# Differential attention: the eight transposes of a query block in one run instead of two groups

## The chip, the cores and the metric

The kernel runs on one core of a Trainium2 chip. The time is the device time of one execution in microseconds (us); where several executions were timed, the median stands for them. The engines are named as in the profile: PE (the matrix engine), PEld (PE's weight loads), DVE (the vector engine), ACT (the scalar engine), POOL and SP (which issues most transfers).

## The reference

A trunk of two layers works on `x` of 1024 positions by 1024 channels. Layer 0 mixes by pooling, layer 1 by differential attention; each is followed by a gated feed-forward part, and a last norm closes it. The change lies in the attention of layer 1, which has 8 heads of two 64-wide halves:

```
sc = jnp.einsum('bqhce,bkhce->bhcqk', qb, k).astype(jnp.float32)
p = jax.nn.softmax(sc, axis=-1)
a = p[:, :, 0] - lam * p[:, :, 1]
return jnp.einsum('bhqk,bkhe->bqhe', a.astype(v.dtype), v)
...
o = _rms_norm(o, subln, DIFF_SUBLN_EPS) * (1.0 - lam_init)
return o.reshape(b, s, h * 2 * dh) @ w_o
```

## The kernel before

Every matrix is split into a high and a low part, and a product is the sum of three products (high by high, high by low, low by high). Names that end in `_hi` and `_lo` are these parts: `_hi` is a rounded copy (L131, on ACT), `_lo` the difference (L132, on DVE).

The attention runs over 8 heads of 8 query blocks of 128 rows, one block a step: 64 steps, and 2 more to drain. A step holds these pieces, each a letter in a string:

- `s`, `S` (`score_mm`): the scores of the first and the second softmax of this block, four matmuls each into a 1024-wide `sc` (L1130); then DVE takes the row maximum (L1132, and a small addition at L1134 for the first), and ACT the exponential with its sum (`prob`, L1135).
- `c` (`combine`): DVE takes a reciprocal (L1141), a factor `cc` (L1143), and puts the two softmaxes together in two halves of 512 columns (L1146).
- `a`, `b` (`a_prep`): the first and the second half of the combined block **of the step before** are transposed on PE, four transposes of 128x128 each (`aT`, L1161), into one PSUM buffer a half; ACT and DVE read it into `a_hi` and `a_lo`.
- `p` (`pv`): on every second step, the product of two blocks with the values (`po`, L1172, 24 matmuls). Its first half needs the halves `a`, its second the halves `b`.
- `t` (`o_turn`): `po` is copied (L1187), transposed (`oT`, L1190), copied (L1191) and squared (L1196).
- `m`, `f`, `F`: the norm of the head before. `m` scales with `rr` (L1210, L1211; the product at L1213 is on POOL), `f` and `F` transpose its output, four transposes each (`oT2`, L1230), only at step 3 of a head.
- `q` (`score_q`): the query parts of the next step, `q_hi` on ACT and `q_lo` on POOL.
- `.`: two matmuls `pj` of the next head's projections (L1041, L1083), in the last head three of the output projection (L1268).

All small transposes and `po` share one PSUM pool of two buffers (tag `tr`): a group waits until the buffer before last has been read.

`PLAN` gives the pieces of an even and an odd step of heads 0 to 6, `PLAN7` those of head 7, the last. The loop is

```
with tc.manual_schedule(engines={mybir.EngineType.PE}):
    for g in range(H * NT + 2):
        j, i = divmod(g, NT)
        pj, pi = divmod(g - 1, NT)
        for step in (PLAN7 if j == H - 1 else PLAN)[g % 2]:
```

so the strings set the order of PE alone. The order of DVE, ACT, POOL and SP is laid out by a scheduler before the run, with its own costs and with priorities that the pieces carry: 20 for the scores and `a_prep`, 50 for `combine` and `o_turn`, 100 for `f` and `F`. Each engine then works through its list in that order.

Of the kernel before, what the change touches and what calls it, by code (L numbers as in the profile page):

```python
# [25 lines left out]
NT = S // P  # L26
NK = D // P
ORDER = (0, 4, 1, 5, 2, 6, 3, 7)
PLAN = ("...saq.bS..c.p", "st.aS.m.q.fb....F.c..")
PLAN7 = (".as.b....S.pqc.", "tmsaSqcb..f......F..")  # L30
AHEAD = 3
WQ, RQ = 14, 3
PB = (2, 1)
# [56 lines left out]
def trunk_kernel(  # L90
# [1233 lines left out]

    assert sum(p.count('.') for p in PLAN) == 18
    done = []
# [4 lines left out]
# [5 lines that stand above are left out]
                if step == ".":  # L1336
# [128 lines left out]
```

## Time and profile before

| | us |
|---|---|
| median of three runs | 2075.68 (2073.62 to 2076.55) |
| the profiled execution | 2073.84 |
| its span, first to last instruction | 2072.0 |
| PE busy | 1998.1 (96%) |
| DVE busy | 1557.2 (75%) |
| ACT busy | 1023.2 (49%) |
| POOL busy | 890.8 (43%) |

The profile is one execution. A row of the timeline has the start, the length in us, the engine, the line and the operation, output from inputs, and, in brackets, how long the engine had been idle and whose end it then followed. A row of waits has the engine and its instruction, the releaser, the us in total, how often, and the longest. The attention steps lie between about 783 and 1350 us; a head's eight steps take 70.4 us, and the steps shown in the prediction (1 to 4 of head 2) begin near 929 us.

### The profile page before, as it was taken

Reading aid. Unit: us, or ns where it says so; the run is one execution under the profiler, and the core shown is the slowest. Engines: PE = TensorE matmul, PEld = TensorE weight load, DVE = VectorE, ACT = ScalarE, POOL = GpSimd, SP = SyncE. Lnnn points to the kernel's source line nnn. Section 1 sums busy time; section 2 is a strip of 40 time slices with the busy share of each in tenths; the row PEclk is TensorE's granted clock in tenths of the full one; section 3 lists DMA queues with packets and bytes.
Section 4 is the critical chain, followed back from the end, with each engine's and each line's share of the span. In section 5 each row is a group of like instructions: output and inputs, shape, how many; then the busy total and the mean of one; then the engine's idle time right before and its main releaser. Section 6 shows DMA issues by size and latency. Waiting matters only on the chain.

```text
span 2072.0 us, 27643 instructions
## 1 busy us (share of the span) xinstructions
PE 1998.1 (96%) x9659; PEld 1664.6 (80%) x9659; DVE 1557.2 (75%) x2286; ACT 1023.2 (49%) x1838; POOL 890.8 (43%) x676
## 2 busy tenths in 40 slices
PE   6699999999999999999999998998999999999998
PEld 6678888888888877888888887876888888888886
DVE  7867777777675658999889988767776777775665
ACT  7733333333453646666667666565433333344343
POOL 4499999996000000101110111015999999930000
PEclk8899999999999999999999999998999999999999
DMA  4325454454976522122212115263445445458663
GB/s 172 104 91 176 138 192 140 158 173 129 378 226 209 193 66 67 43 70 65 64 44 74 56 42 188 102 195 111 130 140 193 147 158 177 138 196 336 201 213 131
DMA packets 221720, 301.90 MB, mean 146 GB/s; under 512 B 17852, under 2 KB 142092, under 8 KB 218764
## 3 DMA queue, kind: packets, MB, share of 16 engines
q1 hardware_dynamic: 221580, 300.13, 44.4%
q8 instruction: 76, 1.25, 0.3%
q14 instruction: 64, 0.52, 0.1%
HBM read 196.78 MB, written 90.70 MB: 139 GB/s over the span
## 4 chain that ended last, share of the span: by engine, by line
PE 87%; DVE 7%; ACT 3%; issue 1%; DMA 1%; SPq 1%; DVEq 0%; ACTq 0%
PE dn L610 19%; PE up_b L436 17%; PE up_c L436 11%; PE up_a L436 11%; PE pj L1041 7%; PE sc L1130 5%; PE pj L1083 4%; PE po L1172 3%; PE aT L1161 3%; PE pj L1268 2%; DVE nm L1132 1%; PE pp L862 1%; ACT prob L1135 1%; PE pl L842 1%; PE wo_acc L1268 1%
## 5 line engine op out<-in xcount | busy, mean ns | idle before, releaser
L1112 POOL TENSOR_TENSOR q_lo<-qt,q_hi 128x256 fp32r<-128x256 f32 x64 | 50.0, 781 | 679.7 <-ACT q_hi L1111 362.2
L394 POOL TENSOR_TENSOR w_lo<-s,w_hi 128x512 fp32r<-128x512 f32 x168 | 269.4, 1604 | 19.4 <-ACT w_hi L393 19.1
L610 PE MATMUL dn<-hnT_hi 128*128 128x512 f32 x560 | 218.3, 390 | 0.0
L610 PE MATMUL dn<-hnT_hi,hnT_lo 128*128 128x512 f32 x560 | 218.1, 389 | 0.0
L610 PE MATMUL dn<-hnT_lo,hnT_hi 128*128 128x512 f32 x560 | 218.1, 389 | 0.0
L436 PE MATMUL up_b<-x_hi,w_hi 128*128 128x512 f32 x528 | 207.5, 393 | 5.0 <-ACT x_hi L318 4.1
L436 PE MATMUL up_b<-x_lo,w_hi 128*128 128x512 f32 x528 | 207.3, 393 | 1.7 <-DVE x_lo L319 1.7
L394 POOL TENSOR_TENSOR w_lo<-raw,w_hi 128x512 fp32r<-128x512 f32 x130 | 194.7, 1499 | 30.8 <-ACT w_hi L393 30.2
L436 PE MATMUL up_b<-x_hi,w_lo 128*128 128x512 f32 x528 | 206.8, 392 | 0.0
L393 ACT CAST w_hi<-s 128x512 fp32r<-128x512 f32 x176 | 108.7, 618 | 178.0 <-PE up_b L436 90.0
L1132 DVE TENSOR_REDUCE nm<-sc 128x1 f32<-128x1024 f32 x128 | 155.8, 1218 | 14.4 <-PE sc L1130 14.0
L593 ACT CAST hnT_hi<-mst 128x1024 fp32r<-128x1024 f32 (+1 forms) x76 | 74.6, 982 | 168.6 <-PE dn L610 128.7
L594 DVE TENSOR_TENSOR hnT_lo<-mst,hnT_hi 128x1024 fp32r<-128x1024 f32 (+1 forms) x76 | 86.5, 1139 | 91.0 <-ACT hnT_hi L593 90.8
L1135 ACT ACTIVATE prob<-sc,nm 128x1024 f32<-128x1024 f32 x128 | 142.7, 1115 | 23.1 <-DVE nm L1132 11.6
L436 PE MATMUL up_a<-hnT_hi,w_hi 128*128 128x512 f32 x352 | 139.2, 396 | 5.3 <-ACT g L513 4.7
L436 PE MATMUL up_a<-hnT_lo,w_hi 128*128 128x512 f32 x352 | 138.6, 394 | 0.1
L436 PE MATMUL up_a<-hnT_hi,w_lo 128*128 128x512 f32 x352 | 138.3, 393 | 0.0
L408 POOL TENSOR_TENSOR s<-raw 128x512 f32<-128x512 f32 x84 | 133.3, 1587 | 11.6 <-DMA raw<-in_ffn_w_up_dram 4.2
L436 PE MATMUL up_c<-hnT_hi,w_hi 128*128 128x512 f32 x352 | 137.3, 390 | 0.0
L436 PE MATMUL up_c<-hnT_hi,w_lo 128*128 128x512 f32 x352 | 137.1, 389 | 0.0
L436 PE MATMUL up_c<-hnT_lo,w_hi 128*128 128x512 f32 x352 | 137.1, 389 | 0.0
L393 ACT CAST w_hi<-raw 128x512 fp32r<-128x512 f32 x132 | 81.6, 618 | 84.8 <-PE up_c L436 76.4
(320 smaller groups left out, 5448.9 us busy)
## 6 DMA issues: line engine op xcount, KB each, us to landing
raw<-in_ffn_w_up_dram SPq DMA_DIRECT2D x88, 512.0 KB, 4.4
mst<-m_dram SPq DMA_DIRECT2D x70, 512.0 KB, 6.2
wd<-in_ffn_w_down_dram SPq DMA_DIRECT2D x22, 1024.0 KB, 6.0
wd_dram<-wd SPq DMA_DIRECT2D x22, 1024.0 KB, 6.4
m_dram<-cm SPq DMA_DIRECT2D x80, 256.0 KB, 5.8
wst<-wd_dram SPq DMA_DIRECT2D x40, 512.0 KB, 5.2
m_dram<-gc SPq DMA_DIRECT2D x66, 256.0 KB, 6.3
wst<-in_ffn_w_down_dram SPq DMA_DIRECT2D x30, 512.0 KB, 5.5
```

The lines of the kernel that those rows point to most:

```text
L393: A.copy(hi, src)
L394: eng.tensor_tensor(lo, src, f32(hi), ALU.subtract)
L408: eng.tensor_tensor(t, a, b, op)
L436: PE.matmul(acc, l[a][:, k], r[b][:, k], start=first and n == 0, stop=n == 11, skip_group_check=True)
L593: A.copy(h_, x)
L594: V.tensor_tensor(l_, x, f32(h_), ALU.subtract)
L610: PE.matmul(banks[t], l[:, q, cols], r[:, q], start=first and cnt == 0, stop=stop and cnt == 3 * n - 1, skip_group_check=True)
L1041: PE.matmul(acc, l[:, k % 2, h], r[:, k], start=(n == 0), stop=(n == 3 * NK - 1))
L1083: PE.matmul(acc, l[:, k % 4], r[:, k], start=(n == 0), stop=(n == 3 * NK - 1))
L1130: PE.matmul(sc[:, ns_], l[:, c], ks[:, c, ns_], start=(l is qhi), stop=(l is qlo))
L1132: V.tensor_reduce(nm, sc, AX.X, ALU.max, negate=True)
L1135: A.activation(soft[j, i][c], sc, AF.Exp, bias=nm, accum_out=sm[:, c, i:i + 1])
```

## The change

In each string the letter `b` moves to stand directly behind `a`:

```diff
-PLAN = ("...saq.bS..c.p", "st.aS.m.q.fb....F.c..")
-PLAN7 = (".as.b....S.pqc.", "tmsaSqcb..f......F..")
+PLAN = ("...sab.qS..c.p", "st.abS.m.q.f....F.c..")
+PLAN7 = (".abs.....S.pqc.", "tmsabSqc..f......F..")
```

On PE, at step 3 of head 2 (`sc` are the scores, `pj` the filler, `aT` the transposes of the combined block, `oT` from `oq` those of the head before), the rows read before:

```order
L1041 MATMUL pj<-hnT_hi_69,wq_hi 128x512
L1161 MATMUL aT<-ident,prob_8463 128x128 x4
L1130 MATMUL sc<-kst,q_hi 128x512 x2
L1130 MATMUL sc<-kst,q_lo 128x512 x2
L1041 MATMUL pj<-hnT_hi_69,wq_lo 128x512
L1041 MATMUL pj<-hnT_lo_70,wq_hi 128x512
L1041 MATMUL pj<-hnT_hi_69,wq_hi 128x512
L1041 MATMUL pj<-hnT_hi_69,wq_lo 128x512
L1041 MATMUL pj<-hnT_lo_70,wq_hi 128x512
L1041 MATMUL pj<-hnT_hi_69,wq_hi 128x512
L1230 MATMUL oT_8598<-ident,oq 128x128 x4
L1161 MATMUL aT<-ident,prob_8463 128x128 x4
```

and now:

```order
L1041 MATMUL pj<-hnT_hi_69,wq_hi 128x512
L1161 MATMUL aT<-ident,prob_8463 128x128 x8
L1130 MATMUL sc<-kst,q_hi 128x512 x2
L1130 MATMUL sc<-kst,q_lo 128x512 x2
L1041 MATMUL pj<-hnT_hi_69,wq_lo 128x512
L1041 MATMUL pj<-hnT_lo_70,wq_hi 128x512
L1041 MATMUL pj<-hnT_hi_69,wq_hi 128x512
L1041 MATMUL pj<-hnT_hi_69,wq_lo 128x512
L1041 MATMUL pj<-hnT_lo_70,wq_hi 128x512
L1041 MATMUL pj<-hnT_hi_69,wq_hi 128x512
L1230 MATMUL oT_8605<-ident,oq 128x128 x4
```

The second four transposes moved from behind `oT` to the first four.

On DVE, between step 2 and step 3 of the same head, the difference of the two orders reads as follows (`nm_8469` and `nm_8500` are the row maxima of step 2, `nm_8546` the first of step 3, `prob_8463` the combined block of step 2):

```order
-L132 TENSOR_TENSOR a_lo<-aT,a_hi 128x4x128
+L132 TENSOR_TENSOR a_lo<-aT,a_hi 128x4x128 x2
 L1134 TENSOR_SCALAR nm_8469<-nm_8469 128x1
 L1132 TENSOR_REDUCE nm_8500<-sc 128x1
-L132 TENSOR_TENSOR a_lo<-aT,a_hi 128x4x128
 L1070 TENSOR_TENSOR kst<-kf,kst 64x512
 L1141 RECIPROCAL r_8507<-sums 128x1
 L1143 SCALAR_TENSOR_TENSOR cc<-sums,neglam,r_8507 128x1
+L1132 TENSOR_REDUCE nm_8546<-sc 128x1
 L1146 SCALAR_TENSOR_TENSOR prob_8463<-prob_8494,cc,prob_8463 128x512 x2
-L1132 TENSOR_REDUCE nm_8546<-sc 128x1
```

Both `a_lo` of step 2 now stand ahead of its second row maximum, and the first row maximum of step 3 stands ahead of the two halves of the combine. Heads 0 to 6 all have this at the turn from step 2 to step 3.

On DVE at the first step of head 7, before:

```order
L1256 SCALAR_TENSOR_TENSOR wo_lo<-hs,subsc,wo_hi 128x1024
L1143 SCALAR_TENSOR_TENSOR cc<-sums,neglam,r_12559 128x1
L1132 TENSOR_REDUCE nm_12605<-sc 128x1
L1146 SCALAR_TENSOR_TENSOR prob_12485<-prob_12517,cc,prob_12485 128x512 x2
L1203 TENSOR_SCALAR vo<-so 128x8
```

and now:

```order
L1143 SCALAR_TENSOR_TENSOR cc<-sums,neglam,r_12559 128x1
L1256 SCALAR_TENSOR_TENSOR wo_lo<-hs,subsc,wo_hi 128x1024
L1146 SCALAR_TENSOR_TENSOR prob_12492<-prob_12517,cc,prob_12492 128x512 x2
L1132 TENSOR_REDUCE nm_12605<-sc 128x1
L1203 TENSOR_SCALAR vo<-so 128x8
```

Here the row maximum moved the other way, behind the combine; farther on, the combine of the next step now stands behind `rr` (L1210). At step 1 of heads 0 to 6 both `a_hi` now stand ahead of ACT's second exponential, and both `a_lo` ahead of the reciprocal (L1141) on DVE. Every engine has the same instructions as before.

## The prediction

> **What bounds the kernel now.** I read the page's busy shares and its chain of waits first, then busy time by stretches of time, then PE's waits, then the timeline round the two groups of transposes.
>
> ```profile
> span 2072.0 us, 27643 instructions
> PE 1998.1 (96%) x9659; PEld 1664.6 (80%) x9659; DVE 1557.2 (75%) x2286; ACT 1023.2 (49%) x1838; POOL 890.8 (43%) x676
> PE 87%; DVE 7%; ACT 3%; issue 1%; DMA 1%; SPq 1%; DVEq 0%; ACTq 0%
> 940.00:1020.00 80.00, 79.50 (x450) 67.04 (x449) 72.98 (x141) 54.58 (x123) 11.32 (x22) 1.00 0.22 60
> PE aT L1161 <- DVE r L1192: 3.1, 6, 0.5
> ```
>
> PE sets the end. In the window row (length, then busy time of PE, its weight loads, DVE, ACT and POOL, then the granted clock) PE works 79.50 of 80 us in the middle of the attention. DVE is close behind with 72.98. So PE has little idle time to give back there, and DVE, which feeds it, has little room to be late. The wait row is the one stall that heads 1 to 6 share: six times PE waits before a group `aT`, up to 0.5 us each.
>
> That stall lies at step 3 of a head. Head 2, before:
>
> ```profile
> 946.16 1.41 DVE L1146 SCALAR_TENSOR_TENSOR prob<-prob,cc,prob 128x512 f32<-128x512 f32 x2
> 946.48 0.63 PE L1130 MATMUL sc<-kst,q_lo 128*128 128x512 f32 x2
> 947.49 1.22 DVE L1132 TENSOR_REDUCE nm<-sc 128x1 f32<-128x1024 f32 x1
> 947.63 0.60 PE L1161 MATMUL aT<-ident,prob 128*128 128x128 f32 x4
> 947.99 0.72 PE L1130 MATMUL sc<-kst,q_hi 128*128 128x512 f32 x2
> 950.39 0.60 PE L1230 MATMUL oT<-ident,oq 128*128 128x128 f32 x4
> 950.66 0.68 DVE L132 TENSOR_TENSOR a_lo<-aT,a_hi 128x512 fp32r<-128x512 f32 x1
> 951.49 0.63 PE L1161 MATMUL aT<-ident,prob 128*128 128x128 f32 x4 [0.50 <-DVE r L1192]
> ```
>
> The combine (two halves, L1146) runs while PE still scores, so its result lies ready when PE comes to the first group at 947.63. The second group comes 3.86 us later, behind `oT2` (L1230), and waits for a PSUM buffer whose old content is read by the `a_lo` at 950.66.
>
> **Removed.** (1) From 950.39 to 951.49 are 1.10 us where a group of four takes 0.36 (947.63 to 947.99). With the second group gone from there, 0.7 us a head go away, six times: **-4.2**. (2) The value product `po` of step 2 stops in its middle for the second group's `a_lo`:
>
> ```profile
> 942.82 0.38 PE L1172 MATMUL po<-a_hi,v_hi 128*128 128x256 f32 x1
> 944.60 0.19 PEld L1172 LDWEIGHTS po<-a_lo,v_hi 128*128 128x128 f32 x1 [0.19 <-DVE a_lo L132]
> 945.90 0.28 PE L1172 MATMUL po<-a_hi,v_lo 128*128 128x256 f32 x1
> 961.80 0.28 PE L1172 MATMUL po<-a_hi,v_hi 128*128 128x256 f32 x1
> 964.55 0.28 PE L1172 MATMUL po<-a_hi,v_lo 128*128 128x256 f32 x1
> ```
>
> That is 3.08 us from first to last against 2.75 at step 4, so 0.33; with both `a_lo` ahead of the next row maximum it goes, seven times (heads 0 to 6): **-2.3**. Nothing else is removed: the instructions are the same, and two groups in one save at most a change of operand that no row shows.
>
> **Added: the first group comes to wait for the combine.** In the changed order DVE has the row maximum of the next score (L1132) ahead of both halves of the combine, in heads 0 to 6 at the turn from step 2 to 3. The trace of before holds this very order once, at the start of head 7:
>
> ```profile
> 1282.01 0.62 PE L1130 MATMUL sc<-kst,q_lo 128*128 128x512 f32 x2
> 1282.25 0.21 DVE L1143 SCALAR_TENSOR_TENSOR cc<-sums,neglam,r 128x1 f32<-128x1 f32 x1
> 1282.67 1.22 DVE L1132 TENSOR_REDUCE nm<-sc 128x1 f32<-128x1024 f32 x1 [0.21 <-PE sc L1130]
> 1283.81 1.40 DVE L1146 SCALAR_TENSOR_TENSOR prob<-prob,cc,prob 128x512 f32<-128x512 f32 x2
> 1284.61 0.87 PE L1161 MATMUL aT<-ident,prob 128*128 128x128 f32 x4 [1.98 <-DVE prob L1146]
> ```
>
> DVE has `cc` at 1282.46 and could combine, but sits idle for 0.21 us until the score ends (1282.63), reduces, and only then combines; PE starts `aT` 1.98 us after the score's end. At step 3 the score ends at 947.11 (946.48 + 0.63) and PE comes to `aT` at 947.63, 0.52 later, with two transposes and two `pj` between. So PE waits 1.98 - 0.52 = 1.46 us. The second group needs the second half: 0.67 us after the first (1.41 for both, less 0.74 for one, 953.73 below), where four transposes take 0.44 (three spacings in the 0.36 of 947.63, so some 0.11 each); another 0.23. Together 1.69 a head, seven times: **+11.8**. The bounds are 0 (the score ends so early that the reduction is over when PE arrives) and 1.98 (nothing between). I take 1.69, since the row is the same pair of instructions in the same order.
>
> **Added: at step 1 everything behind the score comes later.** The second score group `S` now stands behind eight transposes, and ACT does both `a_hi` ahead of its second exponential:
>
> ```profile
> 932.64 0.57 ACT L131 CAST a_hi<-aT 128x512 fp32r<-128x512 f32 x1
> 933.11 0.41 ACT L1111 CAST q_hi<-qt 128x256 fp32r<-128x256 f32 x1
> 933.43 1.12 ACT L1135 ACTIVATE prob<-sc,nm 128x1024 f32<-128x1024 f32 x1
> 937.74 0.17 DVE L1211 TENSOR_TENSOR rr<-rr,r 128x8 f32<-128x8 f32 x1
> 937.98 1.90 POOL L1213 TENSOR_TENSOR oq<-oq,rr 128x1024 f32<-128x1024 f32 x1 [1.63 <-DVE rr L1211]
> 938.46 0.69 DVE L1047 TENSOR_TENSOR t<-pj,cosF 128x512 f32<-128x512 f32 x1 [0.56 <-PE pj L1041]
> 939.66 0.76 DVE L1051 TENSOR_TENSOR t<-t,t 128x512 f32<-128x512 f32 x1
> 940.35 0.68 DVE L1050 TENSOR_TENSOR t<-t,t 128x512 f32<-128x512 f32 x1
> 940.95 1.21 DVE L1132 TENSOR_REDUCE nm<-sc 128x1 f32<-128x1024 f32 x1
> 942.09 0.68 DVE L132 TENSOR_TENSOR a_lo<-aT,a_hi 128x512 fp32r<-128x512 f32 x1
> 1290.11 1.90 POOL L1213 TENSOR_TENSOR oq<-oq,rr 128x1024 f32<-128x1024 f32 x1 [0.30 <-DVE rr L1211]
> 1290.31 1.71 DVE L1143 SCALAR_TENSOR_TENSOR cc<-sums,neglam,r 128x1 f32<-128x1 f32 x1
> ```
>
> One `a_hi` takes 0.47 us from start to start (932.64 to 933.11), so the exponential starts 0.47 later, and with it the reciprocal, the combine, `rr` and POOL's L1213 (937.98). DVE's L1051 starts 0.22 us before that ends and takes 0.76. How DVE fares under POOL's L1213 is seen in the last two rows: `cc`, 0.21 at 1282.25, takes 1.71 and ends with POOL, at 1292.02 against 1292.01. From L1051 on DVE runs without a pause to `a_lo`, for which `po` waits (942.77 and 942.82). So L1213 later by 0.47 puts `po` later by 0.47, six times (head 0 has no L1213): **+2.8**. Bounds: 0, if L1051 isn't held (there is 0.56 us of idle DVE ahead, in which the rest of the delay is lost), and 0.47; I take the upper one, as `cc` shows the hold.
>
> The Trainium skill, "SBUF — State Buffer", "SBUF: two separate sides", has it that an instruction of VectorE with two inputs in SBUF and one of GpSimd exclude each other for the whole of the first. By `cc` the trace agrees; by L1051 only in part: full exclusion would give 0.22 + 0.68 = 0.90 where 0.76 stands. By the rule the term is +2.8 as well; without any exclusion it is 0.
>
> **Elsewhere.**
>
> ```profile
> 953.73 0.74 DVE L1146 SCALAR_TENSOR_TENSOR prob<-prob,cc,prob 128x512 f32<-128x512 f32 x1
> 958.05 0.60 PE L1161 MATMUL aT<-ident,prob 128*128 128x128 f32 x4
> ```
>
> At step 4 the groups start at 958.05, 3.58 us after the second half of step 3 is done (954.47): a combine that comes later by the 1.69 of step 3 stays covered; without that cover it would be as much again. At the start of head 0, where the second group now follows the first at once, I put +0.2 (the 0.23 above). In **head 7** the order goes the other way: the combine now stands ahead of the row maximum, which takes up to 1.46 out of the 1.98 above; but the next combine now stands behind `rr` and so meets L1213, which can hold it as it holds `cc`, by 1.71 - 0.21 = 1.5. I take 0, with -1.46 and +1.5 as the bounds.
>
> **Sum:** -4.2 - 2.3 + 11.8 + 2.8 + 0.2 + 0 = **+8.3 us** on the profiled execution's own 2073.84 (1.84 above its span), which gives 2082.1. The median of the runs, 2075.68, stands 1.84 above that execution, and from it the same sum gives 2084.0; I forecast 2083.0, between them. With the smaller bounds (step 1 at 0, head 7 at -1.46) it is +4.0; with head 7 at +1.5 and step 3 at 1.98 in place of 1.69 (another 2.0) it is +11.8. Its own range is 2079 to 2087.
>
> **Rivals.** *No change* (0.19): the delay at step 1 is lost in DVE's idle 0.56 us and head 7 gains: +4.0, or 2077 to 2079.8. For it: the bounds above; against it: `po` starts only as that `a_lo` ends, already now. *Faster* (0.07): the row maximum ahead of the combine costs nothing, because PE comes to `aT` no sooner than 1.98 us after its score; then only the removed waits are left, -6.5, or 2067 to 2069. The point that decides is the distance from score to `aT`; against it stands 0.52 at 947.63, and nothing in the changed order lies between that didn't before. *Worse* (0.09): DVE, 72.98 of 80 us busy, doesn't catch up behind the new stall, and the combine of head 7 is held by L1213 like `cc` (1.71 - 0.21 = 1.5): +8.3, and 1.5, and the 0.47 of step 1 a second time at a later step of six heads, 2.8: +12.6, or 2086 to 2088.5. *The clock* (0.05):
>
> ```profile
> 1274.00:1278.00 4.00, 2.62 (x19) 2.47 (x20) 4.00 (x6) 2.28 (x4) 0.00 (x0) 1.00 1.03 383
> 1281.00:1284.50 3.50, 1.36 (x6) 0.85 (x6) 3.29 (x6) 1.58 (x6) 0.00 (x0) 1.00 1.05 356
> 1284.50:1288.50 4.00, 3.89 (x14) 3.29 (x15) 3.10 (x8) 2.11 (x4) 1.98 (x10) 0.57 0.95 331
> ```
>
> After the stalls of 1281 to 1284.5 the granted clock was 0.57 for 4 us, which costs about 4 x 0.43 = 1.7 us. If each of seven new stalls brings that, it is 8.3 + 12, about 2095. Against it: 1274 to 1278 has 1.4 us without PE and kept 1.00, and the new stall stands alone in 70 us of full work. The Trainium skill, "TensorE: Matmul & The Clock Gate", "HAM oscillation", sets idle gaps over 3.4 us as the point; its next section tells of a kernel whose clock swung under frequent short gaps, which is this rival. By the first rule there is no dip here; no run here shows yet which holds for one gap of 1.7 us.
>
> **Chances.** The forecast 0.60, the others as given. About 0.2% (4.2 us) is what a measurement of this kernel tells from no change; the forecast's own case, the worse one and the clock lie above it (0.60 + 0.09 + 0.05 = 0.74 slower), the second below (0.19 same), the third gives 0.07 faster. The range 2077 to 2089 takes in the forecast, "worse" and nearly all of "no change": it leaves out some 0.15.
>
> **What would show it.** Right: at step 3 of heads 0 to 6 PE waits about 1.5 us before `aT` for `prob` L1146, some 10 us in all; the six waits on r L1192 are gone; `po` of step 2 runs in 2.75 us; heads 1 to 6 each last some 1.1 us longer. Wrong: `aT` starts about 0.5 us after the score there (DVE's order doesn't bind), or the head period is no longer, or the time turns up in head 7.

## The result and the profile after

| | before | after |
|---|---|---|
| median, us | 2074.65 (2073.47 to 2076.55) | 2095.09 (2094.29 to 2097.62) |
| ratio | | 1.0101 (95% interval 1.009 to 1.0113) |
| profiled execution, us | 2073.84 | 2094.97 |
| its span, us | 2072.0 | 2093.2 |

The change costs 20.4 us, 1.0%. Slower was forecast, with +8.3; the measured time lies above the range. The busy times of the changed kernel:

```profile
PE 1997.3 (95%) x9659; PEld 1663.0 (79%) x9659; DVE 1555.4 (74%) x2286; ACT 1021.1 (49%) x1838; POOL 891.8 (43%) x676
```

Every engine is busy for as long as before, within some 2 us; PE did the same work and stood idle some 22 us more (95.9 against 73.9). PE's waits in heads 0 to 6, after (the instruction, its releaser, us in total, times, longest), say where:

```profile
PE aT L1161 <- DVE prob L1146: 11.0, 8, 2.0
PE aT L1161 <- DVE oTs L132: 10.4, 6, 1.8
PE po L1172 <- DVE a_lo L132: 4.8, 7, 0.7
```

The first row holds the wait that was forecast, 1.29 us in each of seven heads; its eighth, 2.0 us at the very first step, was there before. The second was not forecast at all: the second group of transposes at step 4 waits 1.8 us in six heads for `oTs`, the low part of the turned output of the head before. The third was forecast, but too small (+2.8 us). The wait on `r` L1192 of before is gone.

Step by step, in head 2, from the first score row of a step to that of the next (differences of starts in the timeline of each profiled execution; the runs from `even` on are told below):

| step | before | after | even | odd | keep | ots2q | keepotsq | evenroom | eo | x23 |
|---|---|---|---|---|---|---|---|---|---|---|
| 0 | 7.46 | 7.44 | 7.44 | 7.46 | 7.42 | 7.44 | 7.42 | 7.41 | 7.46 | 7.46 |
| 1 | 9.40 | 9.31 | 9.38 | 9.34 | 9.49 | 9.30 | 9.49 | 9.41 | 9.40 | 9.40 |
| 2 | 7.76 | 8.34 | 7.52 | 8.53 | 8.14 | 8.31 | 8.14 | 10.13 | 10.03 | 7.54 |
| 3 | 11.12 | 12.09 | 12.70 | 10.31 | 11.87 | 12.08 | 11.87 | 14.48 | 11.55 | 11.55 |
| 4 | 7.54 | 9.36 | 7.99 | 8.80 | 9.18 | 7.45 | 7.43 | 7.99 | 7.52 | 7.52 |
| whole head | 70.43 | 73.53 | 72.13 | 71.49 | 73.35 | 71.58 | 71.60 | 76.57 | 73.11 | 70.62 |

After less before is +0.58 at step 2, +0.97 at step 3, +1.82 at step 4 and -0.1 or less at each other step: +3.10 a head, where the prediction's terms make +1.13 (1.69 - 0.7 - 0.33 + 0.47). Heads 1 to 5 agree with head 2 within 0.1 us, but for `odd`, whose heads 4 and 5 are 0.8 and 0.5 longer, and for `evenroom`, where heads 1, 3 and 5 take 74.8 and their step 3 12.7; what sets its head 2 apart is told with that run.

**Step 3** came as foreseen. The timeline of the changed kernel:

```profile
951.86 0.62 PE L1130 MATMUL sc<-kst,q_lo 128*128 128x512 f32 x2
952.52 1.23 DVE L1132 TENSOR_REDUCE nm<-sc 128x1 f32<-128x1024 f32 x1 [0.16 <-PE sc L1130]
953.66 1.41 DVE L1146 SCALAR_TENSOR_TENSOR prob<-prob,cc,prob 128x512 f32<-128x512 f32 x2
954.46 1.38 PE L1161 MATMUL aT<-ident,prob 128*128 128x128 f32 x8 [1.29 <-DVE prob L1146]
```

From the score's end (952.48) to the groups are 1.98 us, the same 1.98 as in the row of head 7 that the prediction took.

**Step 4** is the surprise. Before:

```profile
958.19 0.68 DVE L132 TENSOR_TENSOR oTs<-oT,oTs 128x512 fp32r<-128x512 f32 x1
958.79 1.21 DVE L1132 TENSOR_REDUCE nm<-sc 128x1 f32<-128x1024 f32 x1
959.02 0.63 PE L1161 MATMUL aT<-ident,prob 128*128 128x128 f32 x4
```

After:

```profile
961.15 0.59 SPq L1234 DMA_DIRECT2D oT_dram<-oTs  x1
964.33 0.59 ACT L131 CAST oTs<-oT 128x512 fp32r<-128x512 f32 x1
964.41 0.60 PE L1161 MATMUL aT<-ident,prob 128*128 128x128 f32 x4
964.81 1.22 DVE L1132 TENSOR_REDUCE nm<-sc 128x1 f32<-128x1024 f32 x1
965.94 0.68 DVE L132 TENSOR_TENSOR oTs<-oT,oTs 128x512 fp32r<-128x512 f32 x1
966.77 0.63 PE L1161 MATMUL aT<-ident,prob 128*128 128x128 f32 x4 [1.76 <-DVE oTs L132]
```

The second group takes the PSUM buffer that `F` filled, and must wait until both parts of it are read. Before, they were read ahead of the row maximum of step 4, and the group came at almost the same moment: it starts 0.15 us after the reader's end (958.87 and 959.02), the same 0.15 as after (966.62 and 966.77), so there was no room. After, three things make it wait. The group itself comes some 0.45 us sooner, since no filler stands between it and the first group. There is one SBUF buffer for `oTs`, so ACT can write the second half only when the transfer of the first has left it (issued at 961.15, 3.1 us to landing, written from 964.33). And the row maximum (964.81) now stands ahead of the last reader (965.94) on DVE. Counted from the first score of the step (957.14 before, 963.50 after) ACT's part is 0.44 later and DVE's 1.39, so the row maximum accounts for some 0.95; with the 0.45 that is 1.84, against the 1.82 of the table.

**Step 2** waits for `a_lo` at `po`. The chain from step 1, after:

```profile
940.52 0.74 POOL L1112 TENSOR_TENSOR q_lo<-qt,q_hi 128x256 fp32r<-128x256 f32 x1
940.85 0.42 DVE L1143 SCALAR_TENSOR_TENSOR cc<-sums,neglam,r 128x1 f32<-128x1 f32 x1
943.61 1.90 POOL L1213 TENSOR_TENSOR oq<-oq,rr 128x1024 f32<-128x1024 f32 x1 [2.35 <-DVE rr L1211]
943.98 1.03 PE L1161 MATMUL aT<-ident,prob 128*128 128x128 f32 x8
944.78 1.28 DVE L1051 TENSOR_TENSOR t<-t,t 128x512 f32<-128x512 f32 x1
948.45 0.39 PE L1172 MATMUL po<-a_hi,v_hi 128*128 128x256 f32 x1 [0.70 <-DVE a_lo L132]
```

L1213 starts 0.37 us ahead of the groups of step 2; before it was 1.19 (937.98 and 939.17). It is 0.82 later, not 0.47: ACT's exponential starts 0.54 later against those groups (5.20 ahead of them, before 5.74), `cc` meets POOL's `q_lo` and takes 0.42 in place of 0.21, and the small rest are shifts on DVE, where a filler product (L1047) stands in the place that an `a_lo` had. L1051 takes 1.28 us, held by L1213, and `po` comes 0.82 later too (4.47 behind the groups, before 3.65).

### The profile page after: what moved, and what is told of

The parts are those of the page before. It is cut to its first block, busy times and chain, and to the rows that moved or that the text cites. A ratio compares the mean times of both kernels' runs of the same rounds, so it can differ in the third digit from the quotient of the medians.

```text
span 2093.2 us, 27650 instructions
## 1 busy us (share of the span) xinstructions
PE 1997.3 (95%) x9659; PEld 1663.0 (79%) x9659; DVE 1555.4 (74%) x2286; ACT 1021.1 (49%) x1838; POOL 891.8 (43%) x676
## 4 chain that ended last, share of the span: by engine, by line
PE 85%; DVE 7%; ACT 3%; issue 2%; SPq 2%; DMA 1%; POOL 0%; DVEq 0%; ACTq 0%; POOLq 0%
PE dn L610 19%; PE up_b L436 17%; PE up_c L436 11%; PE up_a L436 11%; PE pj L1041 7%; PE sc L1130 5%; PE pj L1083 4%; PE po L1172 4%; PE aT L1161 2%; PE pj L1268 2%; SPq L1062 1%; PE pp L862 1%; DVE nm L1132 1%; PE pl L842 1%; PE wo_acc L1268 1%
```

## The experiments

Each run is compared with runs of the kernel before on the same chip: the ratio with its interval, and the difference of the medians.

### The strings apart

**even**: the even string alone.

```diff
-PLAN = ("...saq.bS..c.p", "st.aS.m.q.fb....F.c..")
+PLAN = ("...sab.qS..c.p", "st.aS.m.q.fb....F.c..")
```

> Only the even string of heads 0 to 6 changed; the odd string and head 7 as before. Theory of DVE's order (the loss comes from the laid-out order of DVE, where the row maximum of step 3 now stands ahead of the combine): the first group of step 3 waits 1.46 us in seven heads (+10.2), the halt in the middle of `po` at step 2 goes (-2.3), step 4 stays as before: about +8 us. Rival of the PSUM buffers (two groups at once fill both buffers, and whoever comes next waits): the loss sits behind each pair, at even steps only, and step 3 is as before: between +0 and +10, with no wait for `prob` at step 3.

Measured: 1.005 (1.0035 to 1.0065), 10.8 us.

**odd**: the odd string alone.

```diff
-PLAN = ("...saq.bS..c.p", "st.aS.m.q.fb....F.c..")
+PLAN = ("...saq.bS..c.p", "st.abS.m.q.f....F.c..")
```

> Only the odd string of heads 0 to 6 changed. Theory of DVE's order: step 3 has the combine ahead of the row maximum as before, so no wait for `prob` there and the wait behind `f` goes (-0.7 a head); step 1 delays the `po` of step 2 (+0.8 a head); at step 4 the row maximum stands ahead of the `oTs` that frees the buffer for the second group (+1.85 a head): six heads times 1.95, about +12 us. Rival of the PSUM buffers: the same waits would stand at every odd step, 1, 3, 5 and 7; by the trace of the changed kernel steps 5 and 7 didn't lose, so under +5.

Measured: 1.004 (1.0027 to 1.0053), 7.6 us.

PE's waits in the two, first even, then odd:

```profile
PE aT L1161 <- DVE prob L1146: 11.8, 9, 2.0
PE oT L1230 <- DVE oTs L132: 4.1, 6, 0.7
```

```profile
PE aT L1161 <- DVE oTs L132: 8.3, 6, 2.0
PE po L1172 <- DVE nm L1134: 4.1, 7, 0.6
```

The two large waits separate. The even string alone brings the wait for `prob`, at step 3, an odd step whose own string has not changed; so what the first group waits for there isn't the packing but the place of the combine on DVE. Why the scheduler moved the combine isn't shown: in `x23`, below, both `a_lo` of step 2 also stand ahead of the second row maximum, and the combine keeps its place. In the even run `F` waits 0.7 us where the second group did, and step 4 is 0.45 longer, against its expectation; there the reader `oTs` stands ahead of the row maximum (965.57) as before, and only the group comes sooner:

```profile
964.96 0.68 DVE L132 TENSOR_TENSOR oTs<-oT,oTs 128x512 fp32r<-128x512 f32 x1
965.79 0.63 PE L1161 MATMUL aT<-ident,prob 128*128 128x128 f32 x4 [0.37 <-DVE oTs L132]
```

The odd string alone brings the large wait for `oTs` and the late `po`. By the table step 3 of the odd run is 0.81 shorter than before. The rival of the buffers falls: steps 5 and 7 lost nothing. The odd run's step 4 loses 1.26, not 1.85, which is most of the missing 4 us of that forecast.

**seven**: head 7's strings alone.

```diff
-PLAN7 = (".as.b....S.pqc.", "tmsaSqcb..f......F..")
+PLAN7 = (".abs.....S.pqc.", "tmsabSqc..f......F..")
```

> Only head 7's strings changed. From the two traces head 7 begins 21.25 us later and ends 21.1 later, so its own strings give -0.1; theory: within 1.5 us of before, as its gain at the first step is given back at the second. Rival (the strings of head 7 gain and the late start of head 7 in the changed kernel hid it): -2 or more.

Measured: 1.0016 (1.0006 to 1.0026), 3.6 us: neither, it costs. The last `po` of the changed kernel ends 23.0 us later than before (1378.53 against 1355.55), not 21.1, so its trace did hold a loss in head 7. The three ratios less one add up to 1.06%, against 1.01% for the whole change. The changed kernel shows what happens in head 7:

```profile
1301.08 0.70 DVE L1143 SCALAR_TENSOR_TENSOR cc<-sums,neglam,r 128x1 f32<-128x1 f32 x1
1301.70 1.27 DVE L1256 SCALAR_TENSOR_TENSOR wo_lo<-hs,subsc,wo_hi 128x1024 fp32r<-128x1024 f32 x1
1302.90 1.40 DVE L1146 SCALAR_TENSOR_TENSOR prob<-prob,cc,prob 128x512 f32<-128x512 f32 x2
1303.69 1.38 PE L1161 MATMUL aT<-ident,prob 128*128 128x128 f32 x8 [1.92 <-DVE prob L1146]
1312.50 3.04 DVE L1146 SCALAR_TENSOR_TENSOR prob<-prob,cc,prob 128x512 f32<-128x512 f32 x2
1312.66 2.34 POOL L1213 TENSOR_TENSOR oq<-oq,rr 128x1024 f32<-128x1024 f32 x1 [0.55 <-DVE rr L1211]
1315.69 1.09 PE L1161 MATMUL aT<-ident,prob 128*128 128x128 f32 x4 [1.67 <-DVE prob L1146]
```

The combine does stand ahead of the row maximum at the first step, but a `wo_lo` of 1.27 us has taken the row maximum's place between `cc` and the combine, so the wait stays (1.92 against 1.98). At the second step the combine's second half is held by L1213, and the second group waits 1.67. The trace of this run has the same two waits (1.93 and 1.67).

**noseven**: the whole change, but head 7 as before.

```diff
-PLAN7 = (".abs.....S.pqc.", "tmsabSqc..f......F..")
+PLAN7 = (".as.b....S.pqc.", "tmsaSqcb..f......F..")
```

> The changed strings for heads 0 to 6, head 7 as before. Theory: head 7's own strings cost +3.3 by the run with them alone, so this is 3 us below the changed kernel, about +18 against the kernel before. Rival (head 7's strings only cost where heads 0 to 6 keep their pace): +20 or more.

Measured: 1.0105 (1.009 to 1.012), 21.0 us. The interval overlaps that of the whole change almost wholly, so head 7's share inside the changed kernel isn't told by the times. The traces show 2.5 us, 0.4 of them in head 0, whose strings are the same in both: from the first score of head 0 to that of head 7 509.84 against 511.42, and on to the last `po` 84.46 against 85.42.

### The two waits undone, with PE's order kept

**keep**: the first row maximum of a step gets the buffer of `cc`, and so has to wait for the combine of the step before.

```diff
-                nm = small.tile([P, 1], F32, name=f"nm{c}")
+                nm = small.tile([P, 1], F32, name="cc" if c == 0 else "nm1", **({"bufs": 1} if c == 0 else {}))
...
-            cc = small.tile([P, 1], F32, name="cc")
+            cc = small.tile([P, 1], F32, name="cc", bufs=1)
```

> The changed kernel, with the first row maximum of a step written to the buffer that holds the combine's factor `cc`, so that on DVE it has to stand behind both halves of the combine of the step before; PE's order is that of the change. Theory of DVE's order: PE's wait for `prob` at step 3 goes (about 1.7 us in seven heads, -11.9 against the changed kernel), but both row maxima of step 3 now stand ahead of the `a_lo` that frees the buffer for `f`, so some 0.7 us in six heads come back (+4.2); step 4 stays at +1.85: about +13 us against the kernel before. Rival (PE's eight transposes in a row are what costs): no gain, +20.

Measured: 1.0097 (1.0081 to 1.0113), 20.4 us. Its waits:

```profile
PE oT L1230 <- DVE a_lo L132: 4.8, 6, 0.8
PE aT L1161 <- DVE prob L1146: 0.7, 1, 0.7
```

With PE's eight transposes still in a row the wait for `prob` is down from 11.0 to 0.7 us, so it was DVE's order. By the starts of the rows in head 2 the first group of step 3 is 0.18 us late in place of 1.46; the second is still 0.26 late, a cost that only a second group right behind the first has. Of the 1.28 gained, `f`, which now waits for `a_lo`, spends 0.97 again (0.7 was foreseen), so that step 3 gains only 0.22 by the table; and steps 1 and 5 are some 0.2 longer each, which was not foreseen. The time agrees with the rival's figure, the trace with the theory's mechanism.

**ots2q**: a second buffer for `oTs`; the room comes from the turned queries.

```diff
-QT = 5
+QT = 4
...
-            vt = f32(o_p.tile([P, 2, 512], F32R, name="oTs"))[:, 0]
+            vt = f32(o_p.tile([P, 2, 512], F32R, name="oTs", bufs=2))[:, 0]
...
-                oT = o_p.tile([P, 2, 512], F32R, name="oTs") if j < 6 else None
+                oT = o_p.tile([P, 2, 512], F32R, name="oTs", bufs=2) if j < 6 else None
```

> The changed kernel with two buffers in place of one for the turned output of the head before (`oTs`), and four in place of five for the turned queries to make the room; PE's order is that of the change, on DVE the last `oTs` of a head comes to stand ahead of the row maximum of step 4. Theory: the second group of step 4 no longer waits for `oTs`, 1.85 us in six heads, -11 against the changed kernel, so about +10 against the kernel before; step 3 is as in the changed kernel. Rival (the second group waits for DVE in any case, which is behind by the delay of step 3): under -3, so +17 or more.

Measured: 1.005 (1.0035 to 1.0065), 10.1 us, as expected. The row on `oTs` is gone from the waits, that on `prob` stands:

```profile
PE aT L1161 <- DVE prob L1146: 11.5, 9, 2.0
```

Step 4 is 7.45 again. So half of what the change costs hung on `oTs`. How the 1.8 us of step 4 divide wasn't tried by a run of its own, as the second buffer also let the last reader move ahead of the row maximum. The division given above is read from rows; even, in which only the group comes sooner (0.45), and odd, in which only the reader comes later (1.26), bear it out.

**q4**: the changed kernel with `QT = 4` alone.

```diff
-QT = 5
+QT = 4
```

> The changed kernel with four buffers for the turned queries in place of five, nothing else: what the room for the second `oTs` costs by itself. Theory: 0 against the changed kernel, +20 against the kernel before, with the 1.9 us at step 4 still there. Rival (the gain with two `oTs` came from this): step 4 without its wait, +10.

A single execution, 2095.75 us; step 4 takes 9.36 us in head 2, as in the changed kernel, and the wait for `oTs` is again 10.4 us in six. So the gain of ots2q was not from this.

**keepotsq**: both edits together.

```diff
-QT = 5
+QT = 4
...
+            cc = small.tile([P, 1], F32, name="cc", bufs=1)
...
+                oT = o_p.tile([P, 2, 512], F32R, name="oTs", bufs=2) if j < 6 else None
```

> Both of the last two together. Theory: the two losses lie in different steps and add, -7.7 and -11 against the changed kernel: about +2 us against the kernel before. Rival (one delay of DVE that is only moved from step to step): the second remedy adds nothing, +10 or more.

Measured: 1.0033 (1.0019 to 1.0046), 6.2 us. The second remedy brings 14 us on top of keep, so the two waits are not one delay that is passed on; +2 was too low because keep's remedy brings less than was forecast: step 3 is still 0.75 and step 2 0.38 longer than before.

### More room, and versions meant to beat the kernel before

**evenroom**: the even string, with filler moved ahead of the first group at the odd steps.

```diff
-PLAN = ("...saq.bS..c.p", "st.aS.m.q.fb....F.c..")
+PLAN = ("...sab.qS..c.p", "st....aS.m.q.fb.F.c..")
```

> Only the even string changed, and at the odd steps three pieces of filler (six `pj` matmuls of 0.23 us, 1.39 us) moved from behind `f` to ahead of the first group. DVE still has the row maximum ahead of the combine at step 3. Theory: what decides is the distance from the score to the group, which grows from 0.52 to 1.9 us and so covers the 1.98: the wait for `prob` at step 3 all but goes, -9.7 against the run with the even string alone, so about +1 us against the kernel before. Rival (the order on DVE costs wherever the group stands, since everything behind on DVE is late): +8 or more.

Measured: 1.0168 (1.0149 to 1.0188), 33.1 us: far off both. A large part isn't lost at step 3. At step 2, some 2.4 us longer than before in each of heads 1 to 6, `cc` is held under L1213, as in `eo` below, and the groups wait (the first two rows). At step 3 itself the row maximum and the combine stand in the order of the run with the even string alone, and PE comes after the combine:

```profile
943.82 1.88 DVE L1143 SCALAR_TENSOR_TENSOR cc<-sums,neglam,r 128x1 f32<-128x1 f32 x1
946.63 0.63 PE L1161 MATMUL aT<-ident,prob 128*128 128x128 f32 x4 [0.81 <-DVE prob L1146]
956.01 1.23 DVE L1132 TENSOR_REDUCE nm<-sc 128x1 f32<-128x1024 f32 x1 [0.18 <-PE sc L1130]
957.15 1.41 DVE L1146 SCALAR_TENSOR_TENSOR prob<-prob,cc,prob 128x512 f32<-128x512 f32 x2
957.95 0.66 PE L1161 MATMUL aT<-ident,prob 128*128 128x128 f32 x4
963.12 0.69 DVE L1047 TENSOR_TENSOR t<-pj,cosF 128x512 f32<-128x512 f32 x1 [1.85 <-DMA qt<-t]
963.73 0.68 DVE L132 TENSOR_TENSOR oTs<-oT,oTs 128x512 fp32r<-128x512 f32 x1
964.55 1.09 PE L1230 MATMUL oT<-ident,oq 128*128 128x128 f32 x4 [2.28 <-DVE r L1141]
```

No wait is noted at the first `aT` of step 3 (957.95), so the distance does decide there. But the evaluation of the filler (L1047) now stands ahead of `oTs` on DVE, waiting 1.85 us for a transfer; `F` waits behind it. Behind that wait of 2.28 the granted clock fell to 0.57 (964 to 968 us), in head 2 but not in heads 1, 3 and 5, which makes most of the 1.8 by which its step 3 is longer than theirs (by an estimate 4 x 0.43 = 1.7). As a test of the forecast time the run is void.

**bf**: before, with `f` and `b` exchanged.

```diff
-PLAN = ("...saq.bS..c.p", "st.aS.m.q.fb....F.c..")
+PLAN = ("...saq.bS..c.p", "st.aS.m.q.bf....F.c..")
```

> Before, with `f` and `b` exchanged at the odd steps (b directly ahead of f, not behind a). All engines but PE keep the order of before. Theory: the second group no longer waits for the buffer that `f` took, 0.7 us in six heads, and nothing else moves: -4.2 us. Rival (the wait only moves on to the next user of the buffers, `F` or the groups of step 4): 0.

Measured: 1.0001 (0.9992 to 1.001), 0.0 us. The rival was right; the wait stands before the other group now (the row names `r` L1192, which ran last on DVE; the reader of the buffer is the `a_lo` just ahead of it):

```profile
PE oT L1230 <- DVE r L1192: 3.0, 6, 0.5
```

The third group to use two buffers waits for the reader of the first, whichever group it is, and that `a_lo` stands behind a row maximum on DVE.

**eo**: before, with the second score later in both strings.

```diff
-PLAN = ("...saq.bS..c.p", "st.aS.m.q.fb....F.c..")
+PLAN = ("...saq.b.S.c.p", "st.a.S.m.q.fb...F.c..")
```

> The kernel before, with the second score group `S` one piece of filler later in both strings of heads 0 to 6, and the transposes left in two groups. On DVE the `a_lo` of the first group now stands ahead of the second row maximum of step 3, and both `a_lo` of step 2 ahead of its second row maximum; the combine still stands ahead of the first row maximum of step 3, and `oTs` ahead of that of step 4. Theory of DVE's order: both waits of the kernel before go (0.66 us behind `f` in six heads, 0.33 in `po` in seven), -6.3 us. Rival (a later `S` makes the combine late for the next step's groups): 0 or slower.

Measured: 1.008 (1.0067 to 1.0092), 17.1 us, as the rival had it. On DVE `rr` came to stand ahead of the combine of step 1, waits for POOL's small steps, and sets off L1213, under which `cc` takes 1.88 us:

```profile
940.47 0.17 DVE L1210 SCALAR_TENSOR_TENSOR rr<-vo,rs_y 128x8 f32<-128x8 f32 x1 [1.63 <-POOL rs_y L167]
940.92 1.90 POOL L1213 TENSOR_TENSOR oq<-oq,rr 128x1024 f32<-128x1024 f32 x1 [0.48 <-DVE r L1141]
940.95 1.88 DVE L1143 SCALAR_TENSOR_TENSOR cc<-sums,neglam,r 128x1 f32<-128x1 f32 x1
943.76 0.63 PE L1161 MATMUL aT<-ident,prob 128*128 128x128 f32 x4 [1.31 <-DVE prob L1146]
```

**x23**: the later score at steps 2 and 3 alone.

```diff
-            for step in (PLAN7 if j == H - 1 else PLAN)[g % 2]:
+            for step in (PLAN7 if j == H - 1 else ("...saq.b.S.c.p" if i == 2 else PLAN[0], "st.a.S.m.q.fb...F.c.." if i == 3 else PLAN[1]))[g % 2]:
```

> The kernel before, with the second score group `S` one piece of filler later at steps 2 and 3 of heads 0 to 6 alone; every other step, step 1 with its chain through `rr` and POOL among them, keeps its string, and the combine stands where it stood on DVE. Theory: at step 3 the `a_lo` of the first group stands ahead of the second row maximum, so the 0.66 us behind `f` go in six heads; at step 2 both `a_lo` do, so the 0.33 in `po` go in seven; the combine of step 2 comes some 0.5 later and still ends as PE arrives (it ended 0.72 ahead): -6 us. Rival (a later `S` always costs at the next step's groups, as in the run that moved it at every step): 0 or slower.

Measured: 1.0008 (0.9999 to 1.0017), 2.1 us: no gain. Step 2 is 0.22 shorter, the halt in `po` being gone; at step 3, 0.43 longer, the wait behind `f` is gone too, but a new one of 1.07 stands before `F`, which needs the buffer of `f` read out:

```profile
955.21 0.69 DVE L132 TENSOR_TENSOR oTs<-oT,oTs 128x512 fp32r<-128x512 f32 x1
955.95 0.66 PE L1230 MATMUL oT<-ident,oq 128*128 128x128 f32 x4 [1.07 <-DVE oTs L132]
```

No version beat the kernel before.

## Why the prediction was wrong, step by step

- **Direction and first cause: right.** That DVE's row maximum ahead of the combine would hold the first group by 1.46 us at step 3 stands in the trace to the hundredth (1.98 less 0.52), and even and keep show that it is DVE's order. By the starts of the rows (the gap to the first group less the 0.23 of the `pj` ahead, that to the second less 0.11) the first group is 1.46 late and the second 0.26 in each of the seven heads: +12.0 against the term's +11.8.
- **The wait behind `f`, -4.2: right** for the changed kernel (the row is gone). But bf and x23 show that the reason was only half understood: the wait belongs to the turn of two buffers and to `a_lo`'s place on DVE. It went because the changed order puts that `a_lo` ahead of the second row maximum, not because the group moved; in keep, where both row maxima stand ahead of that `a_lo` again, the wait is back (4.8 us, in front of `f`).
- **`po`'s halt, -2.3: right in its place.** `po` runs from 948.45 to the next score at 951.40, 2.95, against 3.20 before (942.82 to 946.02): -0.25 a head, not -0.33.
- **Step 1, +2.8: right mechanism, wrong size.** `po` starts 0.82 us later against its groups, so about +4.9 in six heads. The 0.47 counted ACT's `a_hi` alone, which is 0.54 in the trace; it left out POOL's hold on `cc` (0.21) and the shifts on DVE.
- **"Elsewhere", step 4: the step that failed.** The prediction looked at whether the combine would come in time (3.58 us of cover, and it did), and took that for the only thing the groups wait for. So step 4 stood in the sum at nothing. The second group also needs a PSUM buffer, and the reader of that buffer, `oTs`, had no time to spare even before (read out at 958.87, the group at 959.02). With the group moved up and the reader moved back, step 4 lost 1.82 us a head, six times, about +11. The ots2q run takes out just this.
- **Head 7, 0: too low.** The first step's gain never came, since another long instruction took the place ahead of the combine; the second step's loss was the upper bound's. Behind the second step the granted clock also fell once more than before, 0.51 for 3 us, by an estimate 3 x 0.49 = 1.5 us, which the prediction had counted with the rival alone. Together with the last step of head 6 (9.32 against 8.48) the changed kernel loses some 2.6 us there; seven alone measured 3.6.
- **Sum.** From the first score of head 0 to that of head 7 the traces read 490.15 and 511.42 us: +21.3, where the terms without head 7 gave +8.3. With some 11 for step 4 and 2.1 more for step 1 that is 21.4. That the two agree so well is partly luck: those terms leave out some 1.7 gained in pieces of under 0.1 at steps where nothing was forecast, and 0.8 lost at the last step of head 6 and 0.7 because the halt of `po` gave less than 2.3.
- **The rivals.** The time is that of *the clock* (2095), but by chance: the granted clock was 1.00 from 780 to 1290 us. *Worse* came nearest in kind, a second delay of DVE at a later step of six heads; it named neither the step nor a buffer, and put it at 0.47 where 1.82 was lost. *Faster* and *no change* are out by the interval.

## What to carry to other kernels

Where a scheduler lays out the other engines, a small move on one engine's plan is a move on all: compare the orders of the engines that feed it, and for each instruction that stands later ask who reads its result and who waits for its buffer. A group of instructions waits for its operand and for its destination; a slack found for the one says nothing about the other. And a wait removed at one user of a ring of two buffers is worth nothing while the next user waits for the same reader.

## What the runs showed of the hardware

POOL's L1213 holds DVE's instructions that read two SBUF operands. L1051 starts at 944.78 and ends at 946.06, 0.55 us after L1213 (945.51); before, it ended 0.54 after it (940.42 and 939.88), though the starts lay 1.17 and 1.68 us behind L1213's. L1051 takes 0.68 where L1213 isn't running, so the hold ends, by an estimate from these figures, some 0.13 us before POOL's recorded end. A one-column `cc` takes 0.42 under `q_lo`, 1.71 and 1.88 under L1213, and 0.21 alone. L1047, which reads one operand from PSUM (`pj`), takes its usual 0.69 and 0.68 under L1213 (938.46 and 939.07, before).

The clock did not fall for the new waits at steps 3 and 4 (1.29 and 1.76 us), and it did fall in other places. Windows of the changed kernel (length, PE busy, and, third from the end, the granted clock):

```profile
964.00:968.00 4.00, 2.24 (x15) 1.77 (x14) 3.54 (x9) 2.07 (x5) 0.00 (x0) 1.00 0.26 79
1312.00:1316.00 4.00, 2.02 (x11) 1.32 (x10) 3.85 (x7) 0.59 (x1) 2.45 (x2) 0.94 0.00 0
1316.00:1319.00 3.00, 3.00 (x10) 2.52 (x9) 1.91 (x4) 0.59 (x1) 0.00 (x0) 0.51 0.44 175
780.00:1290.00 510.00, 481.77 (x2695) 407.80 (x2695) 437.73 (x840) 321.62 (x718) 67.06 (x134) 1.00 0.21 57
```

and of `evenroom`, behind its single wait of 2.28 us:

```profile
964.00:968.00 4.00, 3.45 (x11) 2.93 (x12) 3.12 (x7) 0.19 (x1) 0.00 (x0) 0.57 0.35 131
```

In the changed kernel 1.76 us without PE in 4 kept 1.00, and 1.98 in 4, in two waits of which the longer is 1.67, was followed by 0.51; the waits of 1.09 and 1.92 at 1300 to 1304 were followed by 0.60. The length of a wait alone doesn't decide: `evenroom` kept 1.00 behind a single wait of 2.08 us in head 3, and the kernel before kept it behind 0.81 and 2.18 us at 1270 to 1275. What decides is not shown. The Trainium skill, "TensorE: Matmul & The Clock Gate", "HAM oscillation", names idle gaps over 3.4 us; these falls came with no gap that long.
